# The context's first gate and up projection in scaled fp16, with its weight scan moved into the first mixer

## The chip, the cores and the metric

The kernel runs on one core of one Trainium2 chip. The metric is the device time of one execution in microseconds (us). A core has a matrix engine (TensorE: PE for its matmuls, PEld for its weight loads), a vector engine (DVE), an activation engine (ACT), a general engine (POOL) and a queue engine (SP); each runs its own instructions in order and waits on semaphores of the others.

## The reference

Two layers over 1024 latent tokens and 256 context tokens of width 1024. The first layer's mixer is a Fourier part beside a Hyena part, the second's is neighbourhood attention; each layer ends with a SwiGLU feed-forward layer:

```python
def modulate(h, shift, scale):
    return h * (1.0 + scale) + shift

def swiglu(u, w_gate, w_up, w_down):
    return (jax.nn.silu(u @ w_gate) * (u @ w_up)) @ w_down
...
    for i in range(DEPTH):
        ...
        h_lat = h_lat + g1 * y_lat
        h_lat = h_lat + g2 * swiglu(modulate(rms_norm(h_lat, norm2_g[i]), sh2, sc2),
                                    ffn_w_gate[i], ffn_w_up[i], ffn_w_down[i])
        if not last:
            h_ctx = h_ctx + cg1 * y_ctx
            h_ctx = h_ctx + cg2 * swiglu(modulate(rms_norm(h_ctx, norm2_g[i]), csh2, csc2),
                                         ffn_w_gate[i], ffn_w_up[i], ffn_w_down[i])
    return rms_norm(h_lat, final_g)
```

All inputs are float32. The change touches `u @ w_gate` and `u @ w_up` of the context rows in the first layer. w_gate and w_up are 1024 x 2816, which is 22 blocks of 128 columns each.

## The kernel before

Activations lie with channels on the partitions: a block of 128 channels, and pieces of tokens (pieces 0 and 1 are the two halves of the latent tokens, 512 each, piece 2 the 256 context tokens). A float32 product is made from two parts of each factor, high and low, as three products (high-high, high-low, low-high). There are two kinds of parts. In the fp32r kind, `weights` loads a 128x1024 tile on SP's queue, ACT casts the high part (L352) and DVE subtracts for the low part (L354). In the scaled fp16 kind, `weights16` loads the tile and `split_scaled` makes the high part on ACT with a factor (L1933) and the low part on DVE (L1934); the factor is 8192 over the largest magnitude of the whole matrix, so the matrix must have been looked through before. `scale_w` turns column maxima into that factor: POOL reduces over the partitions (`partition_all_reduce`, L1918), DVE takes the maximum, the reciprocal and the product with the activations' own scale. The activations' scale comes from the modulation vectors alone (`scale_x`, L1845 to L1850).

The order of the work is this: first norm, the first mixer's input projection (`in_proj`, into which other work is woven by `weave`-like lists of numbers), the transforms and their inverses, the output projection (`out_proj`, with the function `after1` called when a piece is done), then `ffn`. `ffn` does the context's gate and up first (22 blocks, 48 fp32r matmuls of 256 columns each, L348), beside it the second half of the latent's Winograd sums (`second`), then the latent's gate and up in scaled fp16 with a Winograd scheme (L2080). For the latent's scales, the context's loop lets ACT pass over each loaded weight tile once more (`sums`, L381: Abs with an accumulated sum per partition), and calls `scale_w("here", ...)` behind the last block.

`scan` is the generator for looking through matrices ahead of time: two tiles from the pool S4, for each matrix tile a load issued on ACT's queue and, two steps later, an Abs pass on ACT with accumulation (L1862), each ordered behind a given instruction (`follow`). It is already used for the second layer's gate, up, V, K and Q.

The engines' instruction streams are ordered by a scheduler, which simulates the program; `follow(x)` sets that what is issued within stands behind x. The transform section after `in_proj` has four accumulation pairs whose results DVE combines in chains (L1398 to L1418, then L354), POOL sums (L1275, L1276), ACT casts of transform matrices (`mat`, L402 and L416) and evictions (L1328, L1394).

Of the kernel before, what the change touches and what calls it, by code (L numbers as in the profile page):

```python
# [13 lines left out]
AF = mybir.ActivationFunctionType  # L14
ALU = mybir.AluOpType
AX = mybir.AxisListType.X
MUL, ADD, SUB, MAX, MIN = ALU.mult, ALU.add, ALU.subtract, ALU.max, ALU.min

P = 128
D = 1024  # L20
KB = D // P
LAT = 1024
CTX = 256
NFB = 22
# [234 lines left out]
class Builder:  # L259
# [1650 lines left out]
        self.turn = not getattr(self, "turn", False)  # L1910
        return self.S2() if self.turn else x()

    def scale_w(self, key, groups):

        nc = self.nc
        sums = self.wsc[key]
        n = sums.shape[1] // 2
        nc.gpsimd.partition_all_reduce(sums[:, n:], sums[:, :n], channels=P, reduce_op=bass.bass_isa.ReduceOp.max)  # L1918
        for j, k in enumerate(groups):
            t = self.C(2)  # L1920
            s, inv = t[:, 0:1], t[:, 1:2]
            w = n // len(groups)
            nc.vector.tensor_reduce(s, sums[:, n + j * w:n + j * w + w], axis=AX, op=MAX)
            nc.vector.tensor_scalar(s, s, 1e-30, 1.0 / 8192.0, op0=MAX, op1=MUL)
            nc.vector.tensor_tensor(inv, s, self.xinv, MUL)
            nc.vector.reciprocal(s, s)
            self.wsc[k] = s, inv

    def split_scaled(self, src, t, s):

# [195 lines left out]
    def ffn(self, l, u, h, hs, second, after, keep=None, begun={}):  # L2126

        nc, a = self.nc, self.a
# [26 lines left out]
        hm, raw, inv, dsc = (self.cw[:, c:c + w] for c, w in ((0, n2), (n2, nd), (n2 + 3, nd), (n2 + 6, nd)))  # L2155
        if u is None:
            mx = self.mx
        else:
            wsums = self.C(4 * NFB)
            self.mx = mx = wsums[:, :8 * n2 - 4]  # L2160
        if l == 0:
            self.pad(self.pt, PAD_T)
        if u is not None:
            self.wsc["here"] = wsums
            for fb in range(NFB):
                wide = 3 if fb < NFB - 2 else 2
                gh, gl = self.weights(a["gate"][l, fb], wide=wide, sums=wsums[:, fb:fb + 1])
                uh, ul = self.weights(a["up"][l, fb], wide=wide, sums=wsums[:, NFB + fb:NFB + fb + 1])
                lo = self.last_lo
                ga = self.lin(gh, gl, 0, range(KB), u, (2,))[2]  # L2170
                ua = self.lin(uh, ul, 0, range(KB), u, (2,))[2]
                t = self.T()
                nc.scalar.activation(t[:, :256], ga[:, :256], AF.Silu)
                nc.vector.tensor_tensor(t[:, :256], ua[:, :256], t[:, :256], MUL)
                self.ldr(hidc[fb // 2][:, fb % 2], t[:, :256])
                if fb >= 2:
                    with self.follow(last):
                        next(second, None)
                last = lo
            self.scale_w("here", [(0, 0), (0, 1)])  # L2180
            self.load_cond(act=False)
            todo = self.ada_stream([(l1, m, (0, 1) if l1 == 0 or m < 2 else (0,))
                                    for l1, m in [(0, 5)] + [(1, m) for m in range(6)]], 30)
# [43 lines left out]
        for i in range(NFB // 2):  # L2227
            g, up = begun.get((i, 0)), begun.get((i, 1))
# [12 lines left out]
            if up is None or not up.whole:  # L2241
                wu = self.wino_pair(l, i, 1, up and up.w)
                w = next(wu)
                if up is None:
                    up = Steps(self.wino_steps(w, lambda: self.either(self.TK)))
# [21 lines left out]
            gate = dict(self.res)  # L2267
# [3 lines left out]
            t = self.G()  # L2271
# [15 lines left out]
            for k, t in ks:  # L2287
                sums(k, t)
                if l == 0:
                    x = self.S2()  # L2290
# [15 lines left out]
        ad = self.ada[(l, 0)][:, 40:48]  # L2306
        nc.vector.tensor_scalar(ad, ad, inv[:, 0:1], inv[:, 1:2], op0=MUL, op1=MUL)
        if l == 0:
            nc.vector.tensor_scalar(ad, ad, self.wsc[(0, 1)][1], None, op0=MUL)
            ad = self.ada[(0, 1)][:, 40:48]  # L2310
# [459 lines left out]
    def run(self):  # L2770
        nc, a = self.nc, self.a
# [9 lines left out]
        def drain(g):  # L2781
            for _ in g:
                pass
# [15 lines left out]
        def filters():  # L2799
            gens = [self.filter_raw("l", raws["l"], (o,)) for o in (0, 1)]  # L2800
            next(gens[0])
            yield
            for o in (0, 1):
                tot = self.filter_sum("l", o, raws["l"][o])
                for k, _ in enumerate(gens[o]):
                    if k > 1 and k % 2 == 0:
                        next(tot)
                    yield
                for k, _ in enumerate(self.spectrum_l(o, raws["l"][o], tot)):
                    if o == 0 and k == 5:  # L2810
                        next(gens[1])
                    yield

        long = filters()
        ada = self.late_groups((2, 3), "ws")
        filt = (x for o in (0, 1) for g in (self.filter_raw("c", raws["c"], (o,)), self.spectrum_c(o, raws["c"][o]))
# [4 lines left out]
        def four():  # L2821
            y.t.update(self.new_act(pcs=(2,), blocks=range(4)).t)
            yield from self.fourier_c(y)

        def conv():
            yield from self.forward_c(0)
            yield from self.inverse_c(0, None)
            y.t.update(self.new_act(pcs=(2,), blocks=range(4, 8)).t)
            yield from self.forward_c(1)
            yield from self.inverse_c(1, y)  # L2830

        fc, cc = four(), conv()
        self.in_proj(u, ng, ((long, (1, 2, 4, 5, 5, 5, 5, 5, 6, 0)), (filt, (0,) * 9 + (3, 3, 3, 3, 2)),
                             (ada, (0,) * 5 + (1, 1, 2, 1, 2, 1, 2, 1, 2, 1, 2))), fc, cc)
        self.held = False
        for i in range(8):
            self.tap(f"u{i}", u.ap(0, i, 0))
# [41 lines left out]
        def load_h(pcs):  # L2879
            for pc in pcs:  # L2880
                for b, t in enumerate(self.load_x(pc)):
                    h.put(0, b, pc, t)

        uf = Act()
# [3 lines left out]
        def spill(h, hs, pcs):  # L2888
            for pc in pcs:
                for b in range(KB):  # L2890
                    self.ldr(hs[b][:, pc * 512:pc * 512 + WID[pc]], h.ap(0, b, pc))
# [3 lines left out]
        def after1(pcs):  # L2895
            spill(h, hs0, pcs)
            if 2 in pcs:
                uf.t.update(self.new_act(pcs=(2,)).t)
                rs = self.rms(pcs)
                for b in range(KB):  # L2900
                    self.norm_block({b: h.ap(0, b, 2)}, b, 2, 0, 3, uf, rs[0])
                self.half.add(0)
                self.scale_x(0, 3)
                load_h((1,))
                rest.append(rs[1])
            else:
                drain(first)
                rest.append(self.rms((1,))[0])
# [5 lines left out]

        load_h((2, 0))
        self.out_proj("w_out", y, [(2, 0), (1,)], h, 0, 2, after1, first, late)
        for b in range(8):
            self.tap(f"h1_{b}", h.ap(0, b, 0))
# [37 lines left out]
        ad = self.ada[(1, 0)]  # L2956
# [64 lines left out]
        for i, _ in enumerate(first_part(1)):  # L3021
            if i == 7:
                c = self.rms_begin(0)
# [53 lines left out]
        c = self.rms_begin(1)  # L3077
# [88 lines left out]
```

## Time and profile before

| | |
|---|---|
| three runs | 2812.58, 2817.92, 2819.59 us; median 2817.92 |
| profiled execution | 2812.72 us; span 2810.8 us |
| mean granted TensorE clock | 0.986 |
| instructions | 44489 |
| busy ACT, POOL | 1631.0 us (58%), 514.1 us (18%) |
| DMA | 595.92 MB, mean 212 GB/s |
| issues of the scan's form in the context stage | `s<-in_gate` and `s<-in_up` are loaded by ACT's queue, 22 each of 512 KB |

The span is the time from the first to the last instruction of the profiled execution. Busy times overlap, since the engines run side by side; what an engine's idle time costs is seen only where another engine waits for it. Numbers behind an engine's name in brackets are what ended its idle time ("4.79 <-ACT wh L352": idle for 4.79 us until ACT's write of wh from line 352). Line numbers are those of the kernel before.

### The profile page before, as it was taken

What the parts mean: (1) busy time and instruction counts of PE and PEld (TensorE: products, weight loads), DVE (VectorE), ACT (ScalarE), POOL (GpSimd) and SP (SyncE); (2) the same over time, 40 slices, a digit from 0 to 9 for tenths busy, and PEclk for the clock granted to TensorE, in tenths of its full rate; (3) what the DMA queues carried; (4) which work ended last, traced back from release to release, by engine and by line L of the source; (5) the groups of instructions that cost most, each with busy time, mean ns of one, the idle gap of its engine ahead of it and who ended that gap; (6) DMA issues with size and microseconds to landing.
All of it is one profiled execution on the core that took longest, in us unless ns stands there. A gap on an engine that the chain in (4) does not pass through costs nothing. (4 is left out here: it accounts for less than half of the span.)

```text
span 2810.8 us, 44489 instructions
## 1 busy us (share of the span) xinstructions
PE 2695.3 (96%) x15570; PEld 1717.7 (61%) x15570; DVE 2129.7 (76%) x3870; ACT 1631.0 (58%) x3005; POOL 514.1 (18%) x820
## 2 busy tenths in 40 slices
PE   6999889999999999999999999999989999999998
PEld 3877677878889444444446646767677544444445
DVE  4678788868776899987798646878786877775775
ACT  3533324543487666767556736888774655654653
POOL 2120233351101011122011002333222012221000
PEclk9999899999999999999999999999999999999999
DMA  7244736766655787787988746788955246654863
GB/s 267 95 148 164 226 93 196 232 197 226 213 168 173 244 292 287 284 314 276 360 308 287 238 153 161 193 202 199 253 180 192 89 140 222 224 191 168 296 224 105
DMA packets 312317, 595.92 MB, mean 212 GB/s; under 512 B 83352, under 2 KB 130138, under 8 KB 312094
## 3 DMA queue, kind: packets, MB, share of 16 engines
q1 hardware_dynamic: 241374, 378.61, 42.6%
q0 software_dynamic: 53760, 158.38, 16.3%
q10 hardware_dynamic: 16960, 56.11, 5.8%
q8 instruction: 122, 2.00, 0.3%
q14 instruction: 101, 0.83, 0.1%
HBM read 445.64 MB, written 119.80 MB: 201 GB/s over the span
## 5 line engine op out<-in xcount | busy, mean ns | idle before, releaser
L2080 PE MATMUL ps<-s,s 128*128 128x512 f16 x2280 | 508.9, 379 | 5.6 <-DVE s L2104 3.1
L2080 PEld LDWEIGHTS <-s 128*128 128x128 f16 x2640 | 258.0, 98 | 320.5 <-issue 10.1
L348 PE MATMUL ps<-s,wh 128*128 128x256 f32 (+1 forms) x1784 | 413.8, 334 | 9.3 <-ACT wh L352 6.1
L348 PEld LDWEIGHTS ps<-s,wh 128*128 128x128 f32 x1784 | 300.3, 191 | 44.6 <-ACT wh L352 8.0
L2344 PE MATMUL ps<-s 128*128 128x512 f16 (+2 forms) x1404 | 316.1, 376 | 0.2 <-ACT s L2334 0.2
L2344 PEld LDWEIGHTS <-s 128*128 128x128 f16 x1716 | 166.1, 98 | 196.1 <-issue 5.3
L348 PE MATMUL ps<-s,wl 128*128 128x256 f32 (+1 forms) x892 | 273.0, 332 | 3.2 <-DVE wl L354 3.2
L2334 ACT ACTIVATE s<-s,c 128x512 f16<-128x512 f32 (+1 forms) x300 | 199.9, 714 | 118.7 <-DMA s<-d 63.0
L348 PE MATMUL ps<-s,s 128*128 128x65 f16 (+4 forms) x2748 | 242.4, 238 | 19.3 <-DMA s<-tk 5.0
L2335 DVE SCALAR_TENSOR_TENSOR s<-s,c,s 128x512 f16<-128x512 f32 (+1 forms) x300 | 208.6, 747 | 33.2 <-ACT s L2334 32.7
L339 POOL DMA_DIRECT2D d<-s x245 | 132.9, 544 | 503.6 <-DVE s L2197 170.5
L2080 PE MATMUL ps<-s,hl 128*128 128x512 f16 x924 | 212.2, 379 | 1.2 <-ACT hl L1933 1.2
L348 PE MATMUL pq<-s,hl 128*128 128x512 f16 (+1 forms) x960 | 206.9, 358 | 0.4 <-DVE s L2587 0.4
L348 PEld LDWEIGHTS ps<-s,wl 128*128 128x128 f32 x892 | 168.2, 192 | 21.9 <-DVE wl L354 4.9
L2080 PEld LDWEIGHTS <-hl 128*128 128x128 f16 x1056 | 103.2, 98 | 125.9 <-ACT hl L1933 1.4
L1933 ACT ACTIVATE hl<-ws,c 128x1024 f16<-128x1024 f32 x89 | 101.8, 1144 | 107.8 <-DMA ws<-in_up 37.7
L1934 DVE SCALAR_TENSOR_TENSOR hl<-ws,c,hl 128x1024 f16<-128x1024 f32 x89 | 114.0, 1283 | 62.6 <-ACT hl L1933 62.3
L348 PEld LDWEIGHTS <-s 128*128 128x128 f16 x2400 | 115.2, 98 | 66.8 <-DMA s<-tk 5.7
L348 PEld LDWEIGHTS ps<-s,s 128*128 128x128 f32 (+1 forms) x828 | 128.6, 191 | 35.7 <-PE ps L348 9.5
L1934 DVE SCALAR_TENSOR_TENSOR s<-t,c,s 128x512 f16<-128x512 f32 x176 | 126.6, 747 | 26.3 <-ACT s L1933 26.3
L348 PEld LDWEIGHTS <-hl 128*128 128x128 f16 x960 | 86.8, 98 | 80.3 <-issue 8.8
L1933 ACT ACTIVATE s<-t,c 128x512 f16<-128x512 f32 x176 | 118.1, 714 | 9.2 <-DVE t L2059 5.6
(541 smaller groups left out, 5115.9 us busy)
## 6 DMA issues: line engine op xcount, KB each, us to landing
s<-d SPq DMA_DIRECT2D x326, 256.0 KB, 4.9
d<-s POOLq DMA_DIRECT2D x229, 256.0 KB, 4.5
s<-in_down SPq DMA_DIRECT2D x150, 256.0 KB, 6.4
ws<-in_gate SPq DMA_DIRECT2D x42, 512.0 KB, 4.7
ws<-in_up SPq DMA_DIRECT2D x42, 512.0 KB, 6.0
s<-in_ada_w POOLq DMA_DIRECT2D x34, 512.0 KB, 6.5
d<-s SPq DMA_DIRECT2D x60, 256.0 KB, 2.5
s<-in_ada_w ACTq DMA_DIRECT2D x30, 512.0 KB, 7.4
```

Of the source, the lines that this page charges most:

```text
L339: self.last_ldr = self.nc.gpsimd.dma_start(out, in_).ins
L348: self.last_mm = self.nc.tensor.matmul(o, l, r, start=st, stop=sp).ins
L1933: self.last_hi = self.nc.scalar.activation(hi, src, AF.Copy, scale=s).ins
L1934: self.last_lo = self.nc.vector.scalar_tensor_tensor(lo, src, s, hi, op0=MUL, op1=SUB).ins
L2080: nc.tensor.matmul(ps, x[:, sl], y, start=first and j == 0 and x is wh and y is xh, stop=j == 3 and x is wl, skip_group_check=True)
L2334: self.last_hi = nc.scalar.activation(x, f[:, c:c + 512], AF.Copy, scale=s).ins
L2335: self.last_lo = nc.vector.scalar_tensor_tensor(y, f[:, c:c + 512], s, self.raw_part(x), op0=MUL, op1=SUB).ins
L2344: m = nc.tensor.matmul(acc[j][:, c0:c1], x[:, sl], y[:, xs], start=first and k == 0, stop=last and k == 2, skip_group_check=True)
```

## The change

- The context's gate and up of the first layer are done from scaled fp16 parts: `weights16` instead of `weights`, and the scales are undone in the Silu (`scale=cg`) and in the product (`cu`, a scalar_tensor_tensor).
- The context's activations for it are made as fp16 parts (`new_act16`), and `scale_both(3)` scales the modulation vectors of both the latent and the context, ahead of the context's norm. It takes the place of `scale_x(0, 3)`, which stood behind that norm.
- The Abs passes over the loaded tiles (L381) are gone from the context's loop. The same 44 tiles are loaded once more and looked through by `scan`, woven into `in_proj` from its ninth step on, three steps at a time, the rest drained behind it.
- `scale_w` is divided: its reduction on POOL (`scale_w_begin`) is called behind the scan, the arithmetic on DVE (`scale_w(..., True)`) behind the context's norm statistics, with one factor more for each matrix.

```diff
+    def scale_both(self, m):
+        t, r, s = self.cw[:, 32:36], self.cw[:, 36:40], self.cw[:, 40:42]
+        for c in (0, 1):
+            for j in (0, 1):
+                nc.vector.tensor_reduce(t[:, 2 * j + c:2 * j + c + 1],
+                                        self.ada[(0, c)][:, (m + j) * 8:(m + j) * 8 + 8], axis=AX, op=MAX,
+                                        apply_absolute_value=True)
+        nc.gpsimd.partition_all_reduce(r, t, channels=P, reduce_op=bass.bass_isa.ReduceOp.max)
...
+        for c in (1, 0):
+            ad = self.ada[(0, c)][:, m * 8:m * 8 + 16]
+            nc.vector.tensor_scalar(ad, ad, s[:, c:c + 1], None, op0=MUL)
+    def scale_w_begin(self, key):
+        sums = self.wsc[key]
+        n = sums.shape[1] // 2
+        self.nc.gpsimd.partition_all_reduce(sums[:, n:], sums[:, :n], channels=P, reduce_op=bass.bass_isa.ReduceOp.max)
-    def scale_w(self, key, groups):
+    def scale_w(self, key, groups, both=False):
...
-        nc.gpsimd.partition_all_reduce(sums[:, n:], sums[:, :n], channels=P, reduce_op=bass.bass_isa.ReduceOp.max)
+        if not both:
+            self.scale_w_begin(key)
...
+            if both:
+                self.wsc[k] = s, inv, self.cw[:, 46 + j:47 + j]
+                nc.vector.tensor_tensor(self.wsc[k][2], s, self.xinv_c, MUL)
...
-                gh, gl = self.weights(a["gate"][l, fb], wide=wide, sums=wsums[:, fb:fb + 1])
-                uh, ul = self.weights(a["up"][l, fb], wide=wide, sums=wsums[:, NFB + fb:NFB + fb + 1])
+                gh, gl = self.weights16(a["gate"][l, fb], sg)
+                uh, ul = self.weights16(a["up"][l, fb], su)
...
-                nc.scalar.activation(t[:, :256], ga[:, :256], AF.Silu)
-                nc.vector.tensor_tensor(t[:, :256], ua[:, :256], t[:, :256], MUL)
+                nc.scalar.activation(t[:, :256], ga[:, :256], AF.Silu, scale=cg)
+                nc.vector.scalar_tensor_tensor(t[:, :256], ua[:, :256], cu, t[:, :256], op0=MUL, op1=MUL)
...
-            self.scale_w("here", [(0, 0), (0, 1)])
...
+        sums = self.wsc["here"] = self.C(4 * NFB)
+        scan = self.scan([(a[x][0, fb], sums[:, j * NFB + fb:j * NFB + fb + 1]) for j, x in enumerate(("gate", "up"))
+                          for fb in range(NFB)], lambda: self.last_hi)
...
-                             (ada, (0,) * 5 + (1, 1, 2, 1, 2, 1, 2, 1, 2, 1, 2))), fc, cc)
+                             (ada, (0,) * 5 + (1, 1, 2, 1, 2, 1, 2, 1, 2, 1, 2)), (scan, (0,) * 8 + (3,) * 8)), fc, cc)
+        drain(scan)
+        self.scale_w_begin("here")
...
-                uf.t.update(self.new_act(pcs=(2,)).t)
+                for b in range(0, KB, 2):
+                    uf.t.update(self.new_act16(2, b).t)
+                self.scale_both(3)
                 rs = self.rms(pcs)
+                self.scale_w("here", [(0, 0), (0, 1)], True)
...
-                self.scale_x(0, 3)
```

The scheduler places the new instructions, so the order on the engines says more than the diff. Three places follow; the lines of rows "now" are those of the changed kernel, where L1862, L1275 and L1394 have kept their numbers.

ACT in the transform section, before: `tk` is the copy that the accumulation pairs read, `mat` are transform matrices.

```order
L1288 CAST s_1260_4775<-s_1237_4666 128x1024
L416 CAST mat_4900<-cs_4898 128x1024
L1328 COPY s_1263_4784<-pq_4779 128x512
L1288 CAST s_1264_4786<-s_1258_4769 128x1024
L1394 COPY tk_4868<-ps_4838 128x512
L416 CAST mat_4902<-cs_4898 128x1024
L402 CAST mat_4986<-cs_4984 128x1024
L1394 COPY tk_4922<-ps_4892 128x512
```

These casts and copies stood close behind one another. The same place on ACT now, with the last of the 44 scans (L1862) and the loads ahead of them (L336); the copy `tk` of the first pair stands one row further up:

```order
L416 CAST mat_4994<-cs_4990 128x1024
L402 CAST mat_5078<-cs_5076 128x1024
L1862 ACTIVATE s_781_2870,c_317<-s_781_2870 128x1024
L1288 CAST s_1264_4867<-s_1241_4758 128x1024
L336 DMA s_781_2870<-in_up 128x1024
L1862 ACTIVATE s_782_2871,c_317<-s_782_2871 128x1024
L336 DMA s_782_2871<-in_up 128x1024
L1288 CAST s_1268_4878<-s_1262_4861 128x1024
L1862 ACTIVATE s_781_2870,c_317<-s_781_2870 128x1024
L1862 ACTIVATE s_782_2871,c_317<-s_782_2871 128x1024
L416 CAST mat_5084<-cs_5080 128x1024
L1394 COPY tk_5014<-ps_4984 128x512
```

Between the two copies `tk` of the first and the second accumulation pair now stand four scans and two loads.

POOL in the same section, before: a load for the inverse transform, then the sums of the units.

```order
L339 DMA s_1342_5134<-in_vfo_l 128x1024
L339 DMA s_1343_5136<-in_vfo_l 128x1024
L1526 TENSOR_TENSOR s_963_3607<-t_4829 128x128
L339 DMA s_1347_5154<-in_vfe_l 128x1024
L1275 TENSOR_TENSOR s_1364_5216<-s_1364_5216,s_1365_5217 128x512
L1276 TENSOR_TENSOR s_1364_5216<-s_1364_5216,s_1365_5217 128x512
```

And POOL now; an ISA row that names no tile loads POOL's code.

```order
L339 DMA s_1346_5226<-in_vfo_l 128x1024
L339 DMA s_1347_5228<-in_vfo_l 128x1024
L339 DMA s_1351_5246<-in_vfe_l 128x1024
L1936 ISA
L1936 ISA c_317<-c_317 128x44
L1275 ISA
L1275 TENSOR_TENSOR s_1368_5308<-s_1368_5308,s_1369_5309 128x512
L1276 TENSOR_TENSOR s_1368_5308<-s_1368_5308,s_1369_5309 128x512
```

The reduction of `scale_w_begin` and two loads of code stand between the load of in_vfe_l and the first sum.

DVE before, where the second accumulation pair is taken up:

```order
L1398 TENSOR_TENSOR t_4888<-tk_4868,ps_4839 128x512
L1399 TENSOR_TENSOR t_4889<-tk_4868,ps_4839 128x512
L1525 TENSOR_TENSOR s_963_3607<-t_4829 128x128
L1398 TENSOR_TENSOR t_4942<-tk_4922,ps_4893 128x512
L1399 TENSOR_TENSOR t_4943<-tk_4922,ps_4893 128x512
```

And DVE now:

```order
L1290 TENSOR_TENSOR s_1269_4879<-s_1262_4861,s_1268_4878 128x1024
L1949 TENSOR_REDUCE c_7097<-c_317 128x1
L1949 TENSOR_REDUCE c_7103<-c_317 128x1
L1950 TENSOR_SCALAR c_7097<-c_7097 128x1
L1950 TENSOR_SCALAR c_7103<-c_7103 128x1
L1398 TENSOR_TENSOR t_5034<-tk_5014,ps_4985 128x512
L1399 TENSOR_TENSOR t_5035<-tk_5014,ps_4985 128x512
```

The first instructions of `scale_w`, which the code calls much later, have moved ahead of the second pair's L1398; they read what POOL's reduction writes (c_317).

More of the change, by code (lines that the diff above doesn't have):

```diff
@@ L1911, in either @@
         return self.S2() if self.turn else x()
-    def scale_w(self, key, groups):
+    def scale_both(self, m):
+        nc = self.nc
+        t, r, s = self.cw[:, 32:36], self.cw[:, 36:40], self.cw[:, 40:42]
[5 more added lines that the diff above has]
+        nc.gpsimd.partition_all_reduce(r, t, channels=P, reduce_op=bass.bass_isa.ReduceOp.max)
+        x = self.cw[:, 44:46]
+        nc.vector.scalar_tensor_tensor(x, r[:, 2:4], 32.0, r[:, 0:2], op0=MUL, op1=ADD)
+        nc.vector.tensor_scalar(x, x, 1e-30, 1.0 / 8192.0, op0=MAX, op1=MUL)
+        nc.vector.reciprocal(s, x)
+        for c in (1, 0):
+            ad = self.ada[(0, c)][:, m * 8:m * 8 + 16]
+            nc.vector.tensor_scalar(ad, ad, s[:, c:c + 1], None, op0=MUL)
+        self.xinv, self.xinv_c = x[:, 0:1], x[:, 1:2]
+    def scale_w_begin(self, key):
[3 more added lines that the diff above has]
+    def scale_w(self, key, groups, both=False):
         nc = self.nc
@@ L1925, in scale_w @@
             nc.vector.tensor_tensor(inv, s, self.xinv, MUL)
+            self.wsc[k] = s, inv
+            if both:
+                self.wsc[k] = s, inv, self.cw[:, 46 + j:47 + j]
+                nc.vector.tensor_tensor(self.wsc[k][2], s, self.xinv_c, MUL)
             nc.vector.reciprocal(s, s)
-            self.wsc[k] = s, inv
     def split_scaled(self, src, t, s):
@@ L2158, in ffn @@
         else:
-            wsums = self.C(4 * NFB)
+            wsums = self.wsc["here"]
             self.mx = mx = wsums[:, :8 * n2 - 4]
@@ L2163, in ffn @@
         if u is not None:
-            self.wsc["here"] = wsums
+            (sg, _, cg), (su, _, cu) = self.wsc[(0, 0)], self.wsc[(0, 1)]
             for fb in range(NFB):
-                wide = 3 if fb < NFB - 2 else 2
-                gh, gl = self.weights(a["gate"][l, fb], wide=wide, sums=wsums[:, fb:fb + 1])
-                uh, ul = self.weights(a["up"][l, fb], wide=wide, sums=wsums[:, NFB + fb:NFB + fb + 1])
+                gh, gl = self.weights16(a["gate"][l, fb], sg)
+                uh, ul = self.weights16(a["up"][l, fb], su)
                 lo = self.last_lo
```

## The prediction

> **What bounds the kernel now.** The page was read first: which engine fills the span, and which lines of it.
>
> ```profile
> PE 2695.3 (96%) x15570; PEld 1717.7 (61%) x15570; DVE 2129.7 (76%) x3870; ACT 1631.0 (58%) x3005; POOL 514.1 (18%) x820
> L348 PE MATMUL ps<-s,wh 128*128 128x256 f32 (+1 forms) x1784 | 413.8, 334 | 9.3 <-ACT wh L352 6.1
> ```
>
> TensorE sets the end almost everywhere, so an edit counts by what it does to PE: matmul time, and gaps in front of matmuls. The table by windows and the timeline then cut out the context's gate and up stage, from its first 256-column matmul to the first matmul of the latent gate and up.
>
> ```profile
> 777.54:912.29 134.75, 128.27 (x1068) 127.10 (x1066) 93.86 (x128) 109.80 (x182) 12.36 (x23) 0.97 0.52 166
> 800.00:820.00 20.00, 18.46 (x141) 18.17 (x142) 17.81 (x23) 18.31 (x30) 1.08 (x2) 0.87 0.51 165
> 840.00:860.00 20.00, 20.00 (x172) 20.00 (x171) 15.21 (x18) 17.27 (x29) 1.62 (x3) 1.00 0.50 159
> ...
> 801.07 0.80 PE L348 MATMUL ps<-s,wh 128*128 128x256 f32 x2 [4.79 <-ACT wh L352]
> 912.29 1.04 PE L2080 MATMUL ps<-s,hl 128*128 128x512 f16 x4 [1.22 <-ACT hl L1933]
> ```
>
> Columns of a window: length, then busy time of PE, weight loads (PEld), DVE, ACT and POOL, then the granted clock. In the undisturbed window a matmul takes 20.00/172 = 116.3 ns and weight loading is busy all the time: PE goes at the pace of the fp32r weight loads. The stage has 22 x 48 = 1056 such matmuls, 122.8 us. The other 11.9 us of 134.75 are the stall of 4.79 on ACT's cast at 801.07, the clock of 0.87 after it (2.6 us of that window), the 1.2 us at the end, and a dozen RMS matmuls and small gaps.
>
> **The gain: fp16 instead of fp32r.** These are the engines' groups in that stage, and the latent's fp16 matmuls of the same size (L2469) with the scaled splits that the changed stage will use (L1933, L1934); the last row is a window of L2469 alone.
>
> ```profile
> L381 ACT ACTIVATE t<-s 128x1024 bf16<-128x1024 f32 x44 | 46.0, 1048 | 0.0
> L381 ACT ACTIVATION_READ_ACCUMULATOR t<-s 128x1 f32 x44 | 8.4, 190 | 0.0
> L354 DVE TENSOR_TENSOR wl<-s,wh 128x1024 fp32r<-128x1024 f32 x43 | 52.4, 1223 | 17.0 <-ACT wh L352 13.6 <-DMA ws<-in_up 3.3
> L2174 DVE TENSOR_TENSOR t<-ps,t 128x256 f32<-128x256 f32 x22 | 9.3, 423 | 16.7 <-ACT t L2173 7.1 <-PE ps L348 5.0 <-ACT t L381 4.2
> ...
> L2469 PEld LDWEIGHTS <-hl 128*128 128x128 f16 x528 | 51.6, 98 | 6.8 <-issue 0.8
> L1933 ACT ACTIVATE hl<-ws,c 128x1024 f16<-128x1024 f32 x89 | 101.8, 1144 | 107.8 <-DMA ws<-in_up 37.7 <-PE ps L348 33.8 <-DMA ws<-in_gate 14.3
> L1934 DVE SCALAR_TENSOR_TENSOR hl<-ws,c,hl 128x1024 f16<-128x1024 f32 x89 | 114.0, 1283 | 62.6 <-ACT hl L1933 62.3
> ...
> 1530.00:1540.00 10.00, 10.00 (x94) 8.96 (x92) 1.00 0.84 304
> ```
>
> An fp16 matmul of 256 columns takes 10.00/94 = 106.4 ns, since its weight load (98 ns) hides behind it. So 1056 matmuls save 1056 x 9.9 ns = 10.4 us. The 44 Abs passes leave this stage, 46.0 + 8.4 = 54.4 us of ACT. The stall at 801 came when ACT had run Abs passes one after another ahead of the next cast; with them gone I take the 4.8 us and the clock loss of 2.6 behind it as saved. At the end the scale reduction goes and with it the wait of 1.22, some 1.2 us. I subtract 1.5 us for a start bubble, because the first block's split is now scaled and needs the context's norm in scaled parts. Gain: 10.4 + 4.8 + 2.6 + 1.2 - 1.5 = 17.5 us; bounds 10 (the rate alone) and 19 (no bubble).
>
> What remains must fit a block of 48 x 106.4 ns = 5.1 us. ACT: 2 x 1.144 and a Silu, under 3 us of 5.1. DVE: 2 x 1.283, the product (0.423, costed the same in its scaled form), and the second Winograd stage's work that shares the stage, (93.86 - 52.4 - 9.3)/22 = 1.5 us: 4.5 of 5.1. It fits, with 0.6 us of room. The weights are loaded with the same bytes as before. `scale_both` replaces `scale_x`: two reductions, two small scalings and one wider norm scale more, each under 0.3 us on DVE while the output projection keeps PE busy; its reduction on POOL has the same code load as before (row below), hidden there by the latent part of the projection. I cost it at nothing; if that cover is gone it costs up to the 5.95 us shown below.
>
> **Loss one: 44 scans in the first mixer.** Each is a 512 KB load issued by ACT and an Abs pass with accumulation; the kernel has 68 of the same form elsewhere. The windows are the stretch that takes them: in the changed order 21 scans stand among ACT's work of the first, 23 among that of the second.
>
> ```profile
> L1862 ACT ACTIVATE s<-s 128x1024 f32<-128x1024 f32 x68 | 71.4, 1051 | 14.5 <-DMA s<-in_wq 5.5 <-DMA s<-in_wk 4.5 <-DMA s<-in_gate 2.2
> L1862 ACT ACTIVATION_READ_ACCUMULATOR s<-s 128x1 f32 x68 | 12.9, 190 | 0.0
> ...
> 316.00:456.00 140.00, 121.95 (x610) 101.10 (x611) 117.52 (x274) 41.61 (x85) 39.97 (x48) 0.92 0.49 151
> 456.00:526.00 70.00, 64.46 (x315) 54.13 (x315) 54.64 (x87) 41.94 (x63) 39.34 (x34) 0.92 0.64 199
> 526.00:570.00 44.00, 43.18 (x189) 35.00 (x188) 32.26 (x53) 19.13 (x24) 1.31 (x3) 1.00 0.66 219
> ...
> s<-d SPq DMA_DIRECT2D x10, 512.0 KB, 6.0
> ...
> PE ps L348 <- ACT g L352: 6.3, 3, 2.9
> ```
>
> A scan takes 1.051 + 0.190 = 1.24 us of ACT. In the first window ACT is busy 41.61 of 140 us and 21 x 1.24 = 26 us fit; but ACT runs in order, and a scan whose load has not landed holds the cast behind it. PE already waits there for ACT (the wait row: 6.3 us in three places), so I put 3 us on it, bounds 0 and 6. In the second window ACT has 70 - 41.94 = 28.1 us free and 23 x 1.24 = 28.5 us come in: just full, without any wait for a load. The two tiles also set a pace of their own: a tile is loaded (6.0 us in the DMA row of the second window) and scanned (1.24), so two tiles give one scan in 3.6 us, and 23 of them want 83 us where there are 70. The last loads are issued only a cast and a scan (2.3 us) ahead of their own scans, so ACT will wait some 3.7 of the 6.0 us there. Queued behind the scans on ACT are the casts of the transform matrices (L402, L416), the evictions L1328 and the casts L1288, which PE and DVE consume. Between 0 (the matrices are cast a few microseconds ahead) and 13 (nothing absorbs the slip) I take 6, near the middle, as neither end has a row that favours it. Loss one: 9 us, bounds 0 and 19.
>
> **Loss two: the reduction that DVE waits for.** Behind the scans POOL runs `scale_w_begin`, and DVE the maxima of its result (L1949, L1950), ahead of the second accumulation pair (L1398).
>
> ```profile
> 731.66 0.37 POOL L1846 PARTITION_ALL_REDUCE c<-c  x1 [6.92 <-issue]
> 732.06 0.16 DVE L1847 SCALAR_TENSOR_TENSOR c<-c 128x1 f32<-128x1 f32 x1 [5.95 <-POOL c L1846]
> ...
> 534.40 0.57 POOL L339 DMA_DIRECT2D s<-in_vfe_l  x1 [8.03 <-PE ps L348]
> 569.63 1.29 POOL L1275 TENSOR_TENSOR s<-s,s 128x512 f32<-128x512 f32 x1 [34.66 <-DVE s L1274]
> ...
> 532.42 0.69 DVE L1398 TENSOR_TENSOR t<-tk,ps 128x512 f32<-128x512 f32 x1 [4.99 <-PE ps L348]
> 561.28 0.70 DVE L354 TENSOR_TENSOR s<-g,s 128x512 fp32r<-128x512 f32 x1
> 567.12 1.23 DVE L1269 TENSOR_TENSOR s<-ps,s 128x1024 f32<-128x1024 f32 x1 [5.14 <-PE ps L348]
> ...
> 559.07 0.30 PEld L348 LDWEIGHTS ps<-s,mat 128*128 128x128 f32 x2 [0.44 <-ACT s L352]
> ```
>
> On POOL the reduction stands behind the load of in_vfe_l, which itself waits for PE until 534.40. The other reduction shows the price of switching POOL's code: 6.92 us of issue, and DVE waiting 5.95. So this one ends at about 534.97 + 6.9 + 0.4 = 542.3, and DVE, which before went on at 532.42, is held 10 us. Loading POOL's code back hides in the 34.66 us that POOL idles. DVE then works to 561.98 on that chain almost without a pause, and the loads of weights on TensorE wait at 559.07 for those results by 0.44 us: no slack is left at the end of the chain, and in the window from 526 to 570 PE idles 0.8 us. A shift of 10 therefore passes through almost whole; I take 9 us. Bounds: 0 (PE has other matmuls in that stretch and takes them first) and 13 (9 and a stretch at half clock like the one after 801). If the scans themselves are late, part of this wait is theirs, not a sum.
>
> The Trainium skill ("GPSIMD Engine Reference", section "Instruction dispatch") speaks against the change: the first call of freshly loaded code pays about 6 us with no visible instruction. The trace agrees with 6.92 us here; by the page's figure the term would be 8 instead of 9. The Trainium skill ("TensorE: Matmul & The Clock Gate", section "HAM oscillation") warns of PE gaps over about 3.4 us; the gap of 4.79 and the clock of 0.87 behind it agree, and by that rule a DVE wait that leaves PE one gap of 9 us costs some 2 us more than the gap.
>
> **The sum.** -17.5 + 9 + 9 = +0.5 us. The profiled execution took 2812.72 us (span 2810.8); the three runs shown have their median at 2817.92, 5 us above it, and range over 7 us. So 2813 by the profiled run, and 2818 on the scale of the median; with some overlap of the losses, 2817.
>
> **Rivals.** First, faster: the losses are hidden. ACT is only 42 of 70 us busy, casts run ahead, and PE has matmuls that do not need the held DVE chain. The 68 scans elsewhere cost ACT 14.5 us of waits in all, 0.2 each, which speaks for it; the row at 559.07 speaks against. With losses of 4, the time is 2812.7 - 13.5, about 2804 on the median's scale. Chance 0.31.
>
> Second, slower: the two scan tiles' round trip paces ACT from 456 on. Price: 13 us there, 3 before, and the DVE wait of 10 behind it, 26 - 17.5 = +9 to +14 with a clock loss, 2827 to 2832. It decides once the losses exceed 26 us; the 3.6 us a scan speaks for it, the spacing of the scans elsewhere against. Chance 0.25.
>
> Third, the stage does not reach fp16's pace: DVE's 4.5 of 5.1 us have no room for jitter, blocks stay near the old 5.6 us, and the gain is only 7 us (stall and clock): 2818 + 10 = 2828. Chance 0.06.
>
> The forecast, losses and gain near each other (within 0.3%, 8.4 us, about what a measurement can tell): 0.38. So faster 0.31, same 0.38, slower 0.31. The likeliest case alone spans 2809 to 2826. The range takes in the bounds: low, 2818 - 19 + 3 = 2802; high, gain 14 and losses 32, 2836.
>
> **What would show it.** Right: the context stage lasts 115 to 118 us with matmuls of 106 to 107 ns, PEld under 95%, and no wait of several us on ACT; L1949 on DVE waits about 10 us for POOL near 540, with about 7 us of issue on POOL ahead of the reduction; the scans' idle time by their own loads is over 20 us, and the stretch 316 to 570 grows by 14 to 22 us. Wrong: that stretch grows by under 6 us (first rival) or over 26 (second), or DVE is what PE waits for in the context stage (third).

## The result, and the profile after

The changed kernel took 2832.88 us (median of 6 runs, 2827.71 to 2840.49) against 2815.9 us of the kernel before (6 runs, 2812.58 to 2819.59). The ratio is 1.0057 with a 95% interval of 1.0043 to 1.0071: about 16 us slower. The profiled execution took 2838.17 us with a span of 2836.1. Two rows of its page, and below them the second one of the kernel before (the first is the first row that the prediction shows):

```profile
PE 2701.0 (95%) x15570; PEld 1706.6 (60%) x15570; DVE 2135.3 (75%) x3875; ACT 1638.5 (58%) x3005; POOL 516.1 (18%) x820
q10 hardware_dynamic: 23296, 79.18, 8.2%
...
q10 hardware_dynamic: 16960, 56.11, 5.8%
```

The sums hardly move: ACT has the same number of instructions, since 44 passes have only changed their place. Row q10 is ACT's DMA queue, with 23 MB more. To see where the time went, one takes the matmul of the same number in both traces: the 1180th, 1923rd, 2424th and 3553rd of PE's 15570 bound the projection's second half, the transforms, the units with the output projection (the third stretch), and then the context stage. The order of PE's matmuls is not quite the same, so this matches the amount of work, not each single matmul. The windows between them, in the kernel before (columns: length, busy PE, PEld, DVE, ACT, POOL, granted clock, DMA share, GB/s):

```profile
278.40:454.90 176.50, 153.38 (x744) 123.36 (x743) 149.81 (x338) 57.60 (x113) 46.40 (x60) 0.93 0.53 165
454.90:568.80 113.90, 107.54 (x503) 89.21 (x503) 86.80 (x138) 60.18 (x87) 40.29 (x35) 0.95 0.64 206
568.80:779.07 210.27, 201.08 (x1130) 173.31 (x1130) 159.35 (x294) 92.90 (x146) 61.83 (x77) 0.98 0.64 222
779.07:912.29 133.22, 126.74 (x1056) 125.57 (x1054) 92.33 (x126) 108.28 (x181) 12.07 (x23) 0.97 0.52 166
```

The same four stretches of work in the changed kernel:

```profile
283.90:474.80 190.90, 159.74 (x745) 127.49 (x743) 148.89 (x337) 77.63 (x151) 47.77 (x60) 0.89 0.65 205
474.80:610.90 136.10, 114.92 (x502) 93.99 (x502) 90.78 (x141) 86.22 (x137) 39.91 (x36) 0.89 0.78 267
610.90:823.10 212.20, 201.62 (x1129) 174.71 (x1130) 159.83 (x302) 92.08 (x146) 62.20 (x76) 0.97 0.59 198
823.10:938.60 115.50, 115.50 (x1055) 103.15 (x1054) 94.35 (x117) 72.29 (x95) 11.88 (x22) 1.00 0.72 230
```

The context stage lost 17.7 us (133.2 to 115.5): PE busy without a gap, the clock at 1.00. The projection grew by 14.4 us and the transforms by 22.2. In these two, PE's idle time (length less busy) grew from 23.1 + 6.4 to 31.2 + 21.2 us, 22.9 us in all; the rest is the clock, 0.89 instead of 0.93 and 0.95. Length times the missing clock gives 12 + 6 = 18 us before and 21 + 15 = 36 us now.

The changed kernel's trace is already 5.5 us late where these windows begin (283.9 against 278.4), and the scans have no part in that: their first load is issued at 319.87. Of it some 3 us fall between 270 and 280 us, where the clock was 0.66 against 1.00 before. The profiled executions are also further apart (25 us) than the medians (17).

Who PE waited for in the transforms, in the changed kernel (waits row by row: total us, times, longest):

```profile
PE ps L348 <- ACT s L1288: 4.1, 1, 4.1
PE ps L348 <- ACT s L352: 4.0, 2, 2.4
PE ps L1299 <- DVE s L354: 3.1, 1, 3.1
PE ps L348 <- DVE s L1269: 2.9, 1, 2.9
PE pq L348 <- ACT mat L402: 2.5, 1, 2.5
PE pq L348 <- ACT s L1328: 2.5, 1, 2.5
PE ps L1299 <- ACT s L952: 2.2, 1, 2.2
```

Before there were three rows in that stretch, 4.4, 1.0 and 0.8 us. Now there are ten (the seven largest are shown), none over 4.1 us, for ACT's casts and evictions or for DVE's work. The scans themselves, and the reduction on POOL with DVE behind it, in the changed kernel:

```profile
L1862 ACT ACTIVATE s<-s x44: 1041/1057/1065, 328.5 to 565.9; 128x1024 f32<-128x1024 f32 x44
DMA s<-in_up: 12.2, 9
DMA s<-in_gate: 9.7, 7
...
565.97 0.55 POOL L339 DMA_DIRECT2D s<-in_vfe_l  x1
575.36 0.51 POOL L1936 PARTITION_ALL_REDUCE c<-c  x1 [8.84 <-ACT mat L402]
575.91 0.26 DVE L1949 TENSOR_REDUCE c<-c 128x1 f32<-128x22 f32 x2 [10.35 <-POOL c L1936]
```

ACT sat 21.9 us idle for the scans' loads, and DVE waited 10.35 us for the reduction, which came 8.84 us after POOL was free and some 8 us after the last scan's end at 567.1.

### The profile page after: what moved, and what is told of

The parts are those of the page before. It is cut to its first block, busy times and chain, and to the rows that moved or that the text cites. A ratio compares the mean times of both kernels' runs of the same rounds, so it can differ in the third digit from the quotient of the medians.

```text
span 2836.1 us, 44546 instructions
## 1 busy us (share of the span) xinstructions
PE 2701.0 (95%) x15570; PEld 1706.6 (60%) x15570; DVE 2135.3 (75%) x3875; ACT 1638.5 (58%) x3005; POOL 516.1 (18%) x820
## 5 line engine op out<-in xcount | busy, mean ns | idle before, releaser
L348 PE MATMUL ps<-s,wh 128*128 128x512 f32 (+1 forms) x1080 | 287.1, 367 | 4.3 <-DVE s L844 1.8
L348 PEld LDWEIGHTS <-hl 128*128 128x128 f16 x2016 | 190.1, 98 | 93.5 <-issue 9.5
L2362 DVE SCALAR_TENSOR_TENSOR s<-s,c,s 128x512 f16<-128x512 f32 (+1 forms) x300 | 208.4, 749 | 31.5 <-ACT s L2361 31.2
L1963 DVE SCALAR_TENSOR_TENSOR hl<-ws,c,hl 128x1024 f16<-128x1024 f32 x133 | 170.4, 1284 | 70.2 <-ACT hl L1962 69.8
L348 PEld LDWEIGHTS ps<-s,wh 128*128 128x128 f32 x1080 | 191.0, 191 | 39.6 <-ACT wh L352 4.1
L1962 ACT ACTIVATE hl<-ws,c 128x1024 f16<-128x1024 f32 x133 | 151.5, 1144 | 104.6 <-DMA ws<-in_up 35.5
L2109 PEld LDWEIGHTS <-hl 128*128 128x128 f16 x1056 | 103.2, 98 | 124.6 <-issue 0.8
L348 PE MATMUL ps<-s,wl 128*128 128x512 f32 (+1 forms) x540 | 173.8, 364 | 1.8 <-DVE wl L354 1.8
L1862 ACT ACTIVATE s<-s 128x1024 f32<-128x1024 f32 x112 | 117.9, 1053 | 51.7 <-DMA s<-in_gate 16.5
```

What stands on the lines that cost most here:

```text
L348: self.last_mm = self.nc.tensor.matmul(o, l, r, start=st, stop=sp).ins
L1862: nc.scalar.activation(t, t, AF.Abs, accum_out=tiles[k - 2][1])
L1962: self.last_hi = self.nc.scalar.activation(hi, src, AF.Copy, scale=s).ins
L1963: self.last_lo = self.nc.vector.scalar_tensor_tensor(lo, src, s, hi, op0=MUL, op1=SUB).ins
L2109: nc.tensor.matmul(ps, x[:, sl], y, start=first and j == 0 and x is wh and y is xh, stop=j == 3 and x is wl, skip_group_check=True)
L2362: self.last_lo = nc.vector.scalar_tensor_tensor(y, f[:, c:c + 512], s, self.raw_part(x), op0=MUL, op1=SUB).ins
```

## The experiments

All times are medians; each ratio is to the kernel before, run again beside that experiment, so ratios of different experiments compare better than their medians. The theory after the result was A: the scans hold ACT's in-order stream, above all by the waits for their own loads. Its rival B: DVE's wait of 10 us and the clock behind it make most of the loss.

**Reduction late.** Both calls of the scale arithmetic are put behind a matmul of the output projection. The scheduler still placed POOL's reduction in the transforms (at 569.81 us); DVE's part went to 772.5 us.

```diff
-        self.scale_w_begin("here")
...
-                self.scale_w("here", [(0, 0), (0, 1)], True)
+                with self.follow(self.last_lo):
+                    self.scale_w_begin("here")
+                    self.scale_w("here", [(0, 0), (0, 1)], True)
```

> The changed kernel with DVE's part of the scale reduction (maxima and factors) held back until the output projection; the reduction on POOL stays where it stood, and all scans too. Theory A (the scans on ACT's in-order queue, with waits for their own loads, make most of the loss, and PE's clock drops with the gaps; DVE's wait of 10 us is worth 6 us of it): 2826 us against 2833 of the changed kernel. Theory B (DVE's wait and the clock drops behind it are most of the unforeseen loss): about 2813.

Measured: 2829.0 us, ratio 1.0027 (1.0012 to 1.0043). Against the changed kernel's 1.0057 that is 0.3%, some 8 us by the ratios, whose intervals touch; by the medians and by the length of the transforms (136.1 to 132.2 us) it is 4. So B falls, and the greater part of the loss is elsewhere.

All experiments below have this change in them too, also where an expectation sets them against the first kernel.

**No scans.** On top of that, the scans are gone (`scan = iter(())`) and the sums are set by a memset.

> As the kernel before this one, and all 44 scans with their loads left out; the column sums are set to a constant, so the scales are not those of the weights. The gain of fp16 alone: both theories expect 2816 - 18 = 2798 us. If it comes out above 2806, something else in the change costs time (the scaling of both modulation vectors, the order).

Measured: 2800.31 us, ratio 0.9939 (0.9924 to 0.9954): 17 us by the ratio, 19 by the medians. The gain alone is as forecast. The scans therefore cost 0.9939 to 1.0027, 0.88% or 25 us, and 33 with DVE's wait.

**Four tiles** for the scans instead of two (`range(4)`, pass four steps behind its load).

> As the first kernel, with four tiles instead of two for the scans, so that a load has twice the time before ACT asks for it. Theory A: the waits of ACT for the scans' loads (21.9 us in the changed kernel) fall below 8 us and the time falls by 10 us or more against the first kernel, to about 2815. Rival C (the DMA traffic and the tiles taken from the pool cost the time): no gain, or some us slower than the first kernel, since two more tiles are held.

Measured: 2846.42 us, ratio 1.0101 (1.0077 to 1.0125), slower than with two (reduction late) by some 21 us by the ratios. ACT's waits for the scans' loads fell from 20.7 to about 2 us, and yet the time rose, which speaks against A; but POOL was held in this run too (see the repaired run below).

**No loads** (42 of the 44 left out: `if k < 2` in place of `if k < n`).

> As the first kernel, with the loads of 42 of the 44 scans left out: ACT passes over the same two tiles again and again, so the scales are not those of the weights. ACT's work of 54 us stays, its waits for the loads and 22 MB of DMA go. Theory A: most of the scans' price goes with the waits, 2804 us. If ACT's own passes are the price: 2818 or more.

Measured: 2831.51 us, ratio 1.0052 (1.0034 to 1.007). This run does not tell the theories apart: its trace shows that the scheduler put the reduction on POOL ahead of POOL's work in the transforms.

```profile
457.39 0.53 POOL L339 DMA_DIRECT2D mat<-in_vfe_l  x1 [5.82 <-DVE c L580]
499.74 0.52 POOL L1950 PARTITION_ALL_REDUCE c<-c  x1 [41.83 <-ACT s L1876]
```

POOL stood 41.83 us, in order, behind a reduction that waited for the last scan.

**Short passes**: each pass covers 128 of 1024 columns (`t[:, :128]`); loads and places stay.

> As the kernel with the reduction late, all 44 loads kept and the scans in nearly the same places, but each Abs pass covers 128 of the 1024 columns, so the scales are not those of the weights. ACT spends some 20 us on the scans instead of 54; its waits for the loads stay. Theory A (ACT's waits for the scans' loads): 2824 to 2832, no clear change against 2829. Theory D (new: the passes' own time in front of the casts that PE and DVE wait for, with clock drops behind the gaps): 2812 or less.

Measured: 2823.42 us, ratio 1.0011 (0.9995 to 1.0027): 4.5 us less than with whole passes by the ratios, which their intervals do not separate. ACT was busy 67.6 us instead of 86.4 in the transforms, but its waits for loads rose from 20.7 to 27.4 us in all. D expected 2812 or less and is missed; no clear change, as A expected, is what the intervals allow.

**The first 24 scans** only; constants for the other 20.

```diff
-        scan = self.scan([(a[x][0, fb], sums[:, j * NFB + fb:j * NFB + fb + 1]) for j, x in enumerate(("gate", "up"))
-                          for fb in range(NFB)], lambda: self.last_hi)
...
+        scan = self.scan(todo_w[:24], lambda: self.last_hi)
```

> As the kernel with the reduction late, but only the 24 scans that are woven into the projection's loop; the 20 that were drained behind it, and so fell into the transforms, are left out (constants in their place, so the scales are not those of the weights). The traces so far put 11 to 15 us of lag ahead of 450 us and 20 behind it: 2800 + 12 = 2812 if each half pays for itself; near 2800 if the price is only the crowding behind 450 us; near 2820 if any scan in the projection is dear.

Measured: 2809.15 us, ratio 0.997 (0.9956 to 0.9984). The 24 scans woven into the projection cost 0.31%, 9 us; the 20 drained behind it 0.57%, 16 us. Rows of the second stretch with 44 scans (reduction late), then with 24:

```profile
471.10:603.30 132.20, 113.75 (x501) 93.90 (x501) 90.46 (x138) 86.44 (x137) 39.08 (x36) 0.90 0.80 276
```

```profile
464.50:580.70 116.20, 107.66 (x501) 88.93 (x501) 89.27 (x138) 65.41 (x97) 40.25 (x35) 0.93 0.66 224
```

132.2 and 116.2 us, where the kernel before has 113.9: five scans are left there instead of 25. The two traces make the difference look too large: the first is of the slowest of its ten executions (2836.36 us), the second of the fastest (2801.65), 35 us apart where the medians are 20 apart.

**20 scans in the output projection**: a second `scan` over `todo_w[24:]`, three steps to each weight tile fetched there, drained ahead of the reduction.

> The first 24 scans as in the kernel with the reduction late; the other 20 are issued in the output projection, three to each weight tile fetched, where ACT is busy 39 of 80 us and PE has no gap; nothing is left out. Theory D: the 20 scans cost little there, so it comes out 0 to 6 us above the kernel with 24 scans alone, some 2814, and the whole change comes level with the kernel before or a little faster. If scans cost the same wherever they stand: 2829.

Measured: 2820.11 us, ratio 1.0003 (0.9986 to 1.002). Its trace has the transforms at 116.9 us, as with 24 scans, and the third stretch at 216.6 instead of 208.0. The end of the last scan and what it released, from ACT, POOL, and ACT again:

```profile
776.65 1.06 ACT L1862 ACTIVATE s<-s 128x1024 f32<-128x1024 f32 x1 [1.63 <-DMA s<-in_up]
...
777.90 0.52 POOL L1936 PARTITION_ALL_REDUCE c<-c  x1 [25.57 <-ACT s L1862]
...
794.83 1.15 ACT L1962 ACTIVATE hl<-ws,c 128x1024 f16<-128x1024 f32 x1 [3.57 <-DVE c L1956]
```

The first split of the context stage waited for a factor: the scans ended too late. Until 760 us the scans in the output projection had added no lag to that of the run with 24 scans; by 794 it was 10 us. So the forecast of some 2814 was missed.

**Half later**: the last 20 stepped with the inverse transform's units, two to a unit, then one.

> The first 24 scans as before, the last 20 stepped with the inverse transform's units (two to a unit, then one) instead of all at once behind the projection; nothing is left out. They spread over about 100 us instead of 70. Theory D (crowding): between 2829 and the kernel with scans in the output projection, about 2820. If it comes out at 2829, spreading within the transforms does not help.

Measured: 2834.0 us, ratio 1.0048 (1.0033 to 1.0064). Here too the reduction had slipped among POOL's sums, with a wait of 5.86 us ahead of it.

**Three repaired or new kernels.** In the next three a constant in the last column of the sums, set late (the last tile's maximum is left out), keeps the reduction out of the transforms. First the half spread over the units:

> The last 20 scans spread over the inverse units, as before, with the reduction on POOL kept out of them by a constant in the last column. Theory E: the run at 2834 lost some 10 us at 560 to 600 us to the held POOL, so 2822 now. If spreading in the transforms is dear by itself: 2830 or more.

Measured: 2822.73 us, ratio 1.0027 (1.0015 to 1.0038), 0.21% less than the run before it, about 6 us. The intervals meet at their ends, but the traces agree: the third stretch, where the reduction had stood, took 219.5 us and now 209.1. POOL's hold was real there (theory E). The time is level with all scans drained at once (1.0027), so this spreading does not help; it moved only three of the 44 scans out of the transforms.

Four tiles, repaired:

> Four tiles for the scans as before, with the reduction on POOL kept out of the transforms by a constant in the last column. Theory E (the 2846 us of the first run with four tiles came from POOL, held in order behind a reduction that waited for the last scan): 2825 or less. If the scans in groups of four are themselves the price: 2840 or more.

Measured: 2841.95 us, ratio 1.0099 (1.0084 to 1.0113). E fails here, and the forecast for its opposite holds: scans in groups of four are dear without the held POOL too. In the trace the projection's second half took 198.9 us and the transforms 135.4.

Small loads, whole passes (`self.lda(t[:, :128], tiles[k][0][:, :128])`):

> As the kernel with the reduction late, with the scans' passes whole (54 us of ACT) but each load cut to 128 of 1024 columns (64 KB), so that it lands at once and little traffic is left; the scales are not those of the weights. A constant in the last column keeps the reduction on POOL out of the transforms, where in the runs with four tiles and without loads it stood ahead of POOL's sums (L1275), so those two runs measured a held POOL as well. Theory A (waits for loads): 2808 or less. Theory D (passes in front of casts): 2818 to 2824. The run with short passes took 5.6 us off 2829, so together the two should account for most of 29 us.

Measured: 2826.34 us, ratio 1.0034 (1.0021 to 1.0047), not below the run with full loads (1.0027). The 20 MB of traffic and the landing of whole tiles are not the price. The loads landed in 2.4 us instead of 5.2 and the last scan began at 518 us instead of 563, yet ACT still waited 13.4 us for them (20.7 with whole tiles): A's 2808 is missed by far, but this run does not take the waits to zero. D's 2818 to 2824 is missed upwards as well.

**Loads by SP** instead of ACT (`nc.sync.dma_start`):

> As the kernel with the reduction late, with the 44 loads issued by SP instead of ACT; passes, tiles and bytes are the same. In the traces each issue holds ACT's sequencer 0.33 us (14.7 us in all) and the first one 4 to 5.7 us, until its tile is free; every run with scans lost 3 to 5 us of PE there. Theory F (the issues are a third part of the price on ACT): 2829 - 6 to 10 = 2819 to 2823. If only the passes and the waits for the data count: 2829, or more if the loads now hold back SP's other loads.

Measured: 2825.74 us, ratio 1.0025 (1.0011 to 1.004): no change, F falls. The trace, this one of the fastest of ten executions, has the transforms at

```profile
468.00:596.50 128.50, 111.41 (x503) 90.18 (x504) 90.20 (x136) 86.03 (x137) 40.82 (x37) 0.94 0.81 282
```

so that the growth there by all the scans lies between 14.6 us (here) and 18.3 us (reduction late).

**30 and 14**: 30 scans from the projection on, 14 in the output projection; every scan is made.

> 30 scans from the projection on, 14 in the output projection; nothing left out. The run with 24 and 20 lost 11 us between 760 and 800 us because its last scan ended at 777.6 and the scales came late. With 14 there the last scan should end near 760 and that stall go: 2809 + 3 (six more scans in the transforms) = 2812, faster than the kernel before by some 5 us. If the stall stays: 2820.

Measured: 2815.0 us, ratio 0.9991 (0.998 to 1.0002); 2812 and a gain of 5 us had been expected. The wait for a factor is gone, as forecast. The third stretch:

```profile
589.50:799.50 210.00, 202.01 (x1129) 174.27 (x1130) 159.17 (x303) 107.05 (x174) 62.12 (x77) 0.98 0.68 232
```

It took 210.0 us (before: 210.3), so 14 scans there cost nothing that shows; the transforms, with 11 scans, took 121.0. The same with loads by SP:

> The best placing so far (30 scans from the projection on, 14 in the output projection, reduction late; 2815) with the loads issued by SP; nothing left out. Theory F: 2808 to 2811, faster than the kernel before by over 0.2%. If SP's queue is the worse place: 2815 or more.

Measured: 2815.76 us, ratio 0.9989 (0.9974 to 1.0004): F falls here as well. Both are some 18 us faster than the changed kernel and level with the kernel before; neither is clearly faster than it.

**What follows.** The price goes with the number of scans that stand in a stretch, and with what that stretch can bear. By the traces, 19 or 20 scans in the projection's second half lengthen it by 8 to 13 us (176.5 to 184.6 in the mildest, 189.1 in the run with the reduction late; 198.9 in groups of four); in the transforms 5, 11 and 25 scans make 113.9 into 116.2, 121.0 and 132.2 (24 scans with loads by SP: 128.5); in the output projection 14 cost nothing. In the stretches that pay, PE waits for chains through ACT, DVE and POOL, and each scan ahead of a link delays it, whether ACT works or waits: shorter passes left longer waits. Shown is this dependence on place and number, and that neither traffic, nor whole tiles, nor ACT's issues make the price. That the delay of single links is the mechanism is read from the waits of PE, not isolated. A rival was not tested: with the scans in it the scheduler also puts PE's own work in another order. Of the 501 matmuls of the transforms, 457 work on the same tiles (by name) at the same number in the traces before and after, and all 501 in the run without scans. No run keeps that order fixed.

## Why the prediction was wrong, point by point

The forecast was that gain and losses cancel (+0.5 us, level within 0.3%); the time rose by 0.57%. The gain came as forecast; the losses were 33 us instead of 18, and nearly all of the excess is in loss one.

- **The gain, 17.5 us: right in the sum.** 17.7 by the stage, 17 to 19 by the run without scans. Rows of the changed kernel's context stage:

```profile
L348 PEld LDWEIGHTS <-hl 128*128 128x128 f16 x1043 | 102.1, 98 | 12.3 <-issue 0.6
L1963 DVE SCALAR_TENSOR_TENSOR hl<-ws,c,hl 128x1024 f16<-128x1024 f32 x44 | 56.4, 1285 | 17.3 <-ACT hl L1962 17.1
L2202 DVE SCALAR_TENSOR_TENSOR t<-ps,c,t 128x256 f32<-128x256 f32 x21 | 10.1, 483 | 3.2 <-ACT t L2201 3.2
```

  A matmul takes 115.5/1056 = 109 ns over the stage (107.5 from 840 to 920 us) where 106.4 was taken, so the rate gave 122.8 - 115.5 = 7.3 us instead of 10.4. In return all the other 10.4 us of the 133.2 went, where 4.8 + 2.6 + 1.2 - 1.5 = 7.1 was taken; there was no start bubble. That the sum fits to 0.2 us is partly luck. The scaled product took 483 ns where 423 was taken. DVE is busy 94.4 of 115.5 us and PE waits for it nowhere in the stage: the third rival is out.
- **Loss two, 9 us: right in the mechanism, its price measured only roughly.** 8 us by the ratios, 4 by the medians. DVE's wait is 10.35 us where 10 was worked out, in the place that was named and behind the reduction that was named. With the reduction late DVE still stood 6.79 us at the same place (L1398), for PE.
- **Loss one, 9 us (bounds 0 and 19): mis-sized, the step that failed.** It measured 25 us: 9 for the 24 scans woven into the projection and 16 for the 20 behind it. Two parts of it were too small. For the projection, 3 us (at most 6) was read from the waits of PE on ACT that already were there; the stretch grew by 12.6 us with the reduction late, 14.4 in the changed kernel and 8.1 in the run with loads by SP, above the upper bound each time. For the transforms, 6 us (at most 13) came from ACT's throughput, 28.1 us free against 28.5 wanted, and was the middle of its bounds with no row for it; the stretch grew by 18.3 us with the reduction late and 14.6 with loads by SP, though ACT was busy only 86.4 of 132.2 us in the first of these. For 10 us it was full (9.96 busy from 480 to 490 us in the changed kernel), over the stretch it was not. So the load of ACT is the wrong measure; that its order is the right one is argued from PE's waits.
- **The signs.** The context stage came as forecast (115.5 us, PEld busy 89% of it, no wait), with matmuls at 107.5 instead of 106 to 107 ns. The scans' waits for their own loads, 21.9 us, came as forecast (over 20). The stretch from 316 to 570 us grew by some 32 us, which the prediction had named as the sign of the second rival (over 26).
- **The clock was left out of loss one.** The prediction gave the clock some 2 us behind DVE's wait, and a loss of up to 5 in the second rival. Here a wait of 2.86 us is followed by half the clock:

```profile
510.69 1.63 PE L348 MATMUL ps<-s,mat 128*128 128x512 f32 x3 [2.86 <-DVE s L1269]
...
500.00:507.00 7.00, 7.00 (x35) 5.84 (x33) 2.99 (x3) 2.79 (x6) 3.36 (x2) 1.00 0.97 351
511.00:514.00 3.00, 3.00 (x8) 2.32 (x8) 3.00 (x5) 1.23 (x3) 2.69 (x2) 0.50 0.91 334
515.00:525.00 10.00, 10.00 (x46) 8.21 (x45) 7.56 (x7) 8.58 (x14) 6.24 (x4) 1.00 0.72 236
```

  The Trainium skill ("TensorE: Matmul & The Clock Gate", section "HAM oscillation") warns of gaps over about 3.4 us; in this trace a shorter one is followed by the drop. Even gaps of 1.50 and 1.80 us, ending at 305.03 and 309.45, are followed by 0.50 from 310 to 312.5. The clock took 18 us more than before in the two stretches (overlapping PE's idle time).
- **The second rival** (ACT paced by the tiles' round trip, 2827 to 2832) had the sign and the size, but the runs do not bear out its cause: four tiles removed the waits and made it slower (though they also put the scans together), and small loads, which let the last scan begin 45 us sooner, took the same time.
- **The first rival's evidence**, 0.2 us of wait per scan elsewhere, came from stretches where PE hardly waits for ACT: 0.8 us from 940 to 1320 us and 1.7 from 1565 to 1660, in the kernel before.

## What to carry to other kernels

Work that is moved off a bound engine's stage must be priced at the place where it lands by the chains there, not by the idle share of the engine that takes it: here ACT was 33 to 53% busy, and 25 us went. Where PE waits on chains of short steps, count the clock too: here 22.9 us of new gaps came with 13.8 us of longer busy time for the same number of matmuls. A small reduction can hold two in-order queues; see where the scheduler puts it and its consumer (41.83 us of POOL without loads, 10.35 us of DVE in the changed kernel).

## What the runs showed of the hardware

- The first DMA issue of the scans held ACT's sequencer for 4.55 us in the changed kernel, others 0.33 us, and a copy behind it that PE waited for came 3.44 us late:

```profile
319.87 4.55 ACTq L336 DMA_DIRECT2D s<-in_gate  x1
324.46 0.58 ACT L1058 COPY s<-pq 128x512 f32<-128x512 f32 x1 [3.44 <-issue]
```

  What it was held by the trace does not say, and that it waited for its tile is not shown. In the run with all 44 loads by SP no issue took over 0.75 us, and the scans cost the same within the intervals.
- Executions of one kernel lie up to 18 us apart: 2819.83 to 2836.36 over ten with the reduction late, 2810.61 to 2828.18 over 23 of the kernel before. So stretches of two single traces differ for other reasons than the edit too: the clock from 270 to 280 us, before any scan, was 1.00 in one trace and 0.66 in the other, behind gaps of 1.49 and 1.61 us.
